# The 96-column matmuls of the 96 + 32 expert units issued as three of 32 columns

## The chip, the cores and the metric

The kernel runs on one core of a Trainium2 chip. The metric is the device time of one execution in microseconds, as the median of several runs.

## The reference, cut to what matters

One layer of a diffusion backbone: 512 latent tokens and 256 context tokens of width 1024 go through a modulated norm, an input projection, two scans (SSD and mLSTM) in both directions and an output projection; then the latent tokens alone go through a mixture of 32 experts, of which each token uses two. The change touches the experts only:

```
g_sel = jnp.argmax(g_logits, axis=-1)                      # one group of 8 experts per token
top_logit, top_idx = lax.top_k(e_logits, MOE_TOP_K)        # two experts inside it
...
hidden = silu(einsum("td,edf->tef", t, w_gate[lo:hi])) * einsum("td,edf->tef", t, w_up[lo:hi])
hidden = hidden * combine[:, grp, :, None]
y = y + einsum("tef,efd->td", hidden, w_down[lo:hi])
```

An expert is a gate and an up matrix of 1024 x 256 each and a down matrix of 256 x 1024, all in float32.

## The kernel before

After the scans and the router, the kernel knows how many tokens each expert has. It ranks the experts by that, and gives them places in 14 units of 128 rows (`plan`, line 40, `SEQ_U`, line 59): a P or M unit holds two experts with 64 rows each, a B unit one with 128, a C unit two with 96 and 32, a Q unit four with 32 each. The order is P P P M C B M C Q B M C Q Q, units 0 to 13; a table says which token stands in which row, and rows that stay empty give nothing. Tokens that find no place go through a loop of extra tiles (line 1331), which runs as often as it is needed.

The loop over the units (line 1410) does the following for each. POOL gathers the 128 token rows into `xg` (line 1413). The unit's experts' weights are tiles `we` of 128 x 2048 float32, 1 MB, three to an expert: two hold gate and up for half of the depth each, the third the down matrix. `load_unit` (line 931) issues them on SP's queue, through `piece` (line 908), in the order first tiles, second tiles, third tiles of all the unit's experts. There are 20 slots for such tiles; a load waits until the slot's last reader is done, and until the load two before it has landed. So SP runs ahead of PE by up to 20 tiles. The last unit's down matrices come in narrower pieces (`piece_cols`, line 922).

Line 1416 makes `halves`: for each expert of the unit a triple of its weight tiles, the first of its rows and their number. `moe_tile` (line 1263) then computes the unit. PE transposes `xg` (tile `xt`, line 1269); DVE and ACT scale it into `xT` (tokens along the columns). For each of the eight blocks k of the depth, and for each entry of `halves`, one matmul (line 1279) takes the entry's columns of `xT` as the stationary operand and 512 columns of its weight tile as the moving one, and adds into the entry's rows of `gu`: gate on the left, up on the right. ACT and DVE make `hid` of it, PE transposes that, and the down matmuls (line 1313, tile `yy`) go in the same way over two halves of the output and two blocks q of the hidden width, again one for each entry of `halves`. Every float32 matmul shows in the trace as two instructions with two weight loads. DVE scales the result (`yf`), ACT and DVE split it into `yH` and `yL`, and the scatter matmuls (lines 1299 and 1300, tile `pa`) with a one-hot matrix bring the rows back to token order, where DVE adds them to `x1t`. PE does the scatter of one unit between the matmuls of the next.

Of the kernel before, what the change touches and what calls it, by code (L numbers as in the profile page):

```python
# [82 lines left out]
def body(tc, a, out, dbg=None):  # L83
# [28 lines left out]
    def mps(name):  # L112
        return pmix.tile([128, 512], F32, name=name, tag="mx", bufs=3)
# [526 lines left out]
    for c in (5, 4, 3, 2, 1, 0):  # L640
        o = (c % 4) * 128
# [289 lines left out]
    def load_unit(es, last):  # L931
        ws = [[None] * 3 for _ in es]
        for t in range(3):
            for w, e in zip(ws, es):
                w[t] = piece(e, t, LASTC if last and t == 2 else None)
        if last:
            for c0, cn in LASTC:
                for w, e in zip(ws, es):
                    piece_cols(w[2], e, c0, cn)
        return ws  # L940
# [238 lines left out]
    def gather(xg, idx):  # L1179
        G.indirect_dma_start(out=xg, out_offset=None, in_=xnd, in_offset=bass.IndirectOffsetOnAxis(ap=idx, axis=0), bounds_check=SEQ - 1, oob_is_err=False)  # L1180
# [78 lines left out]
    def onehot(n, tokf):  # L1259
        oh_ = mw.tile([128, SEQ], F32R, name=f"oh{n}", tag="oh", bufs=1)  # L1260
        return oh_, ts(oh_, iota, tokf, None, ALU.is_equal)
# [65 lines left out]
    def rank_exp(r):  # L1327
        return SY.value_load(ordi[0:1, r:r + 1], min_val=0, max_val=NE - 1)
# [81 lines left out]
    for i, unit in enumerate(UNITS):  # L1410
        oh_ = None
        if i:
            gather(xgs[0], tabi[:, i:i + 1])
            oh_ = onehot(i, tabf[:, i, 0:1])[0]
        ws = [pre[r] for r, _, _ in unit] if unit[0][0] < NP else load_unit([rank_exp(r) for r, _, _ in unit], i == NU - 1)
        halves = [(w.__getitem__, p0, m) for w, (_, p0, m) in zip(ws, unit)]
        if i == NU - 1:
            fw = slots[npc[0] % NSLOT][0].tile([128, 2048], F32, name="fw", tag="we", bufs=1)
            fwr = fw[0:1, D:2 * D]
            S.dma_start(fwr, a["fw"])  # L1420
            for nb in range(2):
                pf_ = mps(f"pfw{nb}")
                T.matmul(pf_, ones[0:1], fwr[:, nb * 512:nb * 512 + 512], start=True, stop=True)
                S.copy(fw[:, nb * 512:nb * 512 + 512], pf_)
        moe_tile(i, xgs[0], oh_, tabf[:, i, 1:2], halves, last=i == NU - 1)
# [85 lines left out]
```

## Time and profile before

| | us |
|---|---|
| median of 3 runs | 796.37 |
| lowest, highest | 796.34, 801.81 |
| span of the profiled execution | 795.4 |
| of it PE busy with matmuls | 729.2 |
| DVE busy | 411.7 |
| ACT busy | 267.2 |
| POOL busy | 139.5 |
| mean granted clock of PE | 0.970 of full speed |

The profiled span goes from the first to the last instruction of one execution; it lies 1.0 us below the median of the timed runs. The expert stage fills the time from about 455 us to the end. "PE" is the matmuls, "PEld" their weight loads, which can run beside them; "SPq" is what SP's DMA queue issues. In a shape such as `128*96 128x512`, 128 is the depth of the matmul, 96 the number of stationary columns (rows of the result), and 512 the moving columns.

### The profile page before, as it was taken

The numbers are of one execution on the slowest core, as the hardware profiler recorded it, in microseconds if no ns is written. First come the engines' busy times: TensorE is split into PE (matmuls) and PEld (weight loads), VectorE is DVE, ScalarE is ACT, GpSimd is POOL, SyncE is SP. The second block draws the span as 40 slices with busy tenths as digits, with TensorE's granted clock in tenths as the row PEclk, the third lists the DMA queues.
The fourth block names the chain that finished last, engine by engine and source line by source line (L and its number), as shares of the span: only waits on it lengthen the run. The fifth ranks groups of instructions, "written<-read, shape, count | busy, mean of one in ns | idle before, by whom it ended". The sixth has DMA issues, their size and how long they took to land.

```text
span 795.4 us, 10678 instructions
## 1 busy us (share of the span) xinstructions
PE 729.2 (92%) x3941; PEld 427.2 (54%) x3941; DVE 411.7 (52%) x872; ACT 267.2 (34%) x576; POOL 139.5 (18%) x142
## 2 busy tenths in 40 slices
PE   5998999999989999999989578999999999999883
PEld 3554544446768888999978433333343234323321
DVE  3557594124565757349886834444353245434415
ACT  6235215212644684642444411221122112202224
POOL 3110000201386420136560100000000000000002
PEclk9999999999999999999999779999999999999997
DMA  8765367210514831152485579988668579893722
GB/s 354 251 240 226 131 214 267 70 36 31 183 52 165 306 139 54 54 207 87 162 314 246 214 298 399 362 320 316 241 220 333 216 268 340 318 386 131 270 101 105
DMA packets 36648, 171.59 MB, mean 216 GB/s; under 512 B 4643, under 2 KB 7283, under 8 KB 23796
## 3 DMA queue, kind: packets, MB, share of 16 engines
q1 hardware_dynamic: 32912, 162.68, 55.0%
q0 software_dynamic: 2592, 6.30, 2.2%
q10 hardware_dynamic: 1092, 1.93, 0.8%
q8 instruction: 31, 0.51, 0.2%
q14 instruction: 21, 0.17, 0.1%
HBM read 169.74 MB, written 4.30 MB: 219 GB/s over the span
## 4 chain that ended last, share of the span: by engine, by line
PE 82%; DVE 7%; ACT 5%; issue 2%; POOL 2%; DMA 1%; another core or an unknown queue 0%; SPq 0%; DVEq 0%; ACTq 0%; POOLq 0%
PE gu L1279 17%; PE sx L256 10%; PE yy L1313 10%; PE z L256 5%; PE pa L1299 4%; PE pa L1300 3%; PE o L256 3%; PE op L256 3%; PE oq L256 3%; PE xm L256 2%; PE v L256 2%; PE py L704 2%; PE modl L578 2%; PE xm_c L256 1%; PE mod L277 1%
## 5 line engine op out<-in xcount | busy, mean ns | idle before, releaser
L1279 PE MATMUL gu<-we,xT 128*32 128x512 f32 (+3 forms) x512 | 140.9, 620 | 1.0 <-DVE xT L121 1.0
L116 DVE TENSOR_TENSOR x1t<-x1t,pa 128x512 f32<-128x512 f32 (+1 forms) x116 | 72.0, 665 | 44.4 <-PE pa L1300 44.4
L1313 PE MATMUL yy<-we,hTm 128*32 128x512 f32 (+4 forms) x272 | 80.2, 592 | 1.9 <-ACT hTm L1291 1.0
L1279 PEld LDWEIGHTS gu<-we,xT 128*32 128x32 f32 (+3 forms) x512 | 35.5, 132 | 82.7 <-issue 79.8
L1180 POOL DMA_INDIRECT xg<-xnd,tabi x14 | 14.2, 1013 | 266.3 <-PE xt L1269 243.6
L1299 PE MATMUL pa<-yH,oh 128*128 128x512 f32 (+1 forms) x116 | 47.7, 468 | 3.3 <-ACT yH L1318 2.6
L1284 ACT ACTIVATE hid<-gu 128x256 f32<-128x256 f32 x14 | 5.4, 384 | 124.7 <-PE gu L1279 124.7
L1318 ACT CAST yH<-yf 128x512 fp32r<-128x512 f32 (+1 forms) x29 | 17.5, 603 | 86.0 <-DVE yf L116 86.0
L1313 PEld LDWEIGHTS yy<-we,hTm 128*32 128x32 f32 (+3 forms) x272 | 20.6, 130 | 46.0 <-issue 39.3
L124 DVE SCALAR_TENSOR_TENSOR hid<-hid,tabf,gu 128x256 f32<-128x256 f32 x14 | 6.7, 480 | 72.6 <-ACT hid L1284 72.6
L124 DVE SCALAR_TENSOR_TENSOR cv<-sx,pc,cv 128x510 f32<-128x510 f32 (+1 forms) x32 | 23.8, 744 | 30.3 <-ACT cv L454 29.8
L1300 PE MATMUL pa<-yL,oh 128*128 128x512 f32 (+1 forms) x116 | 39.4, 397 | 0.0
L1275 ACT ACTIVATE xT<-xt,mv,mv 128x128 f32<-128x128 f32 x84 | 32.1, 455 | 20.0 <-DVE xT L121 20.0
L1299 PEld LDWEIGHTS pa<-yH,oh 128*128 128x128 f32 x116 | 20.4, 188 | 33.0 <-ACT yH L1318 12.4
L116 DVE TENSOR_TENSOR yf<-yy,g2b 128x512 f32<-128x512 f32 (+1 forms) x29 | 19.4, 670 | 35.8 <-PE yy L1313 35.5
L226 POOL TENSOR_TENSOR w_1L<-w,w_1H 128x1024 fp32r<-128x1024 f32 x5 | 12.1, 2424 | 131.7 <-ACT w_1H L222 131.7
L1319 DVE TENSOR_TENSOR yL<-yf,yH 128x512 fp32r<-128x512 f32 (+1 forms) x29 | 19.5, 672 | 13.0 <-ACT yH L1318 12.9
L1300 PEld LDWEIGHTS pa<-yL,oh 128*128 128x128 f32 x116 | 20.5, 188 | 9.0 <-DVE yL L1319 3.1
L1269 PE MATMUL xt<-ident,xg 128*128 128x128 f32 x112 | 19.6, 289 | 4.4 <-issue 4.4
L692 ACT ACTIVATE sg<-sg,cu 128x128 f32<-128x128 f32 x64 | 19.6, 389 | 9.1 <-POOL sg L629 9.1
L226 POOL TENSOR_TENSOR w_0L<-w,w_0H 128x1024 fp32r<-128x1024 f32 x3 | 7.2, 2412 | 86.4 <-ACT w_0H L222 86.4
L256 PE MATMUL sx<-hH,w_0H 128*128 128x512 f32 x32 | 19.5, 620 | 3.1 <-DVE cv L124 2.0
(515 smaller groups left out, 1701.6 us busy)
## 6 DMA issues: line engine op xcount, KB each, us to landing
we<-in_wex_dram SPq DMA_DIRECT2D x92, 1024.0 KB, 6.0
wl<-in_w_mod_dram SPq DMA_DIRECT2D x16, 1024.0 KB, 5.2
w<-in_win_dram SPq DMA_DIRECT2D x24, 512.0 KB, 6.5
wm<-in_wm_dram SPq DMA_DIRECT2D x8, 1024.0 KB, 10.1
sg<-rowS SPq DMA_DIRECT2D x8, 512.0 KB
sw<-rowS SPq DMA_DIRECT2D x8, 512.0 KB, 7.8
xin<-in_x_dram SPq DMA_DIRECT2D x4, 512.0 KB
mg<-rowM SPq DMA_DIRECT2D x4, 512.0 KB
```

Of the source, the lines that this page charges most:

```text
L116: return (eng or V).tensor_tensor(o, x, y, op)
L124: return V.scalar_tensor_tensor(o, x, s, y, o1, o2)
L226: wsub[0] = G.tensor_tensor(wL, raw, wH, ALU.subtract)
L256: T.matmul(ps, l, r, start=(start and i == 0), stop=(stop and i == n - 1))
L692: S.activation(gb[:, h], gb[:, h], AF.Exp, bias=cu[:, c, 12 * d + h:12 * d + h + 1])
L1269: T.transpose(pt[:, q * 128:(q + 1) * 128], xg[:, k * 128:(k + 1) * 128], ident)
L1275: S.activation(xT[:, k], pt[:, q * 128:(q + 1) * 128], AF.Identity, bias=B2[:, k:k + 1], scale=A2[:, k:k + 1])
L1279: T.matmul(gu[p0:p0 + m], xT[:, k, p0:p0 + m], w(k // 4)[:, (k % 4) * 512:(k % 4) * 512 + 512], start=(k == 0), stop=(k == KB - 1))
L1299: T.matmul(pa, osl, yH, start=True, stop=False)
L1300: T.matmul(pa, osl, yL, start=False, stop=True)
L1313: T.matmul(py[p0:p0 + m], hT[:, q, p0:p0 + m], w(2)[:, q * D + c0:q * D + c0 + cn], start=(q == 0), stop=(q == 1))
L1319: V.tensor_sub(yL, yf, yH)
```

## The change

Line 1416 makes more entries for `halves`. An expert with 96 rows in its unit (only the first of a C unit has that) gives three entries of 32 rows, at its first row and at 32 and 64 rows behind it, all with the same weight tiles. Experts with 128, 64 or 32 rows give one entry as before. `moe_tile` is not changed: it issues one matmul for each entry, at lines 1279 and 1313.

```
-        halves = [(w.__getitem__, p0, m) for w, (_, p0, m) in zip(ws, unit)]
+        halves = [(w.__getitem__, p0 + o, min(m, q_)) for w, (_, p0, m) in zip(ws, unit) for q_ in ((32 if m == 96 else 128),) for o in range(0, m, q_)]
```

## Rows read from the trace of the kernel before

**Rows 1.** The page, part 1: engine, busy us (share of the span), instructions.

```profile
PE 729.2 (92%) x3941; PEld 427.2 (54%) x3941; DVE 411.7 (52%) x872; ACT 267.2 (34%) x576; POOL 139.5 (18%) x142
```

**Rows 2.** Chain of waits from 455 us on, shares by line.

```profile
by line: PE gu L1279 40.0%; PE yy L1313 22.7%; PE pa L1299 9.0%; PE pa L1300 7.9%; PE xt L1269 2.6%; DVE hid L124 2.0%; PE ph L1288 1.9%; issue 1.7%; ACT hTm L1291 1.6%; ACT hid L1284 1.5%; DVE yf L116 1.1%; another core or an unknown queue
```

**Rows 3.** Timeline, PE: first `gu` rows of units; start, us, line, tiles, shape, count.

```profile
544.09 5.03 PE L1279 MATMUL gu<-we,xT 128*96 128x512 f32 x10
...
574.28 2.74 PE L1279 MATMUL gu<-we,xT 128*128 128x512 f32 x6
...
611.24 5.03 PE L1279 MATMUL gu<-we,xT 128*96 128x512 f32 x10
...
641.52 2.76 PE L1279 MATMUL gu<-we,xT 128*32 128x512 f32 x18
...
661.18 2.74 PE L1279 MATMUL gu<-we,xT 128*128 128x512 f32 x6
...
698.16 5.03 PE L1279 MATMUL gu<-we,xT 128*96 128x512 f32 x10
...
728.44 1.06 PE L1279 MATMUL gu<-we,xT 128*32 128x512 f32 x6
...
751.17 1.04 PE L1279 MATMUL gu<-we,xT 128*32 128x512 f32 x2
```

**Rows 4.** Timeline, PE's weight loads inside unit 4, a C unit.

```profile
557.89 0.24 PEld L1279 LDWEIGHTS gu<-we,xT 128*96 128x96 f32 x2 [0.84 <-issue]
558.92 0.14 PEld L1279 LDWEIGHTS gu<-we,xT 128*32 128x32 f32 x2 [0.78 <-issue]
559.89 0.24 PEld L1279 LDWEIGHTS gu<-we,xT 128*96 128x96 f32 x2 [0.84 <-issue]
```

**Rows 5.** Timeline, PE's weight loads inside unit 8, a Q unit.

```profile
648.37 0.13 PEld L1279 LDWEIGHTS gu<-we,xT 128*32 128x32 f32 x4 [0.30 <-issue]
...
648.79 0.13 PEld L1279 LDWEIGHTS gu<-we,xT 128*32 128x32 f32 x4 [0.30 <-issue]
```

**Rows 6.** Chain of waits in order of time: start, us, what; units 4, 8.

```profile
544.25 4.87 PE gu L1279 x10
...
550.51 2.00 PE gu L1279 x4
552.98 9.01 PE gu L1279 x18
...
563.91 7.11 PE yy L1313 x14
...
641.60 2.69 PE gu L1279 x18
...
645.89 0.99 PE gu L1279 x8
...
647.55 4.51 PE gu L1279 x38
...
653.99 3.62 PE yy L1313 x26
```

**Rows 7.** Line 1279, its weight loads: min/median/max in ns, starts, shapes.

```profile
L1279 PEld LDWEIGHTS gu<-we,xT x512: 106/136/230, 462.6 to 765.1; 128*32 128x32 f32 x80, 128*64 128x64 f32 x65, 128*96 128x96 f32 x16, 128*128 128x128 f32 x10
```

**Rows 8.** Line 915, the weight tiles' loads from issue to landing.

```profile
DMA to landing us min/median/max: 4.8/6.0/9.0
```

**Rows 9.** Timeline: SP's queue over two stretches, and `yy` of unit 12.

```profile
704.00 42.09 SPq L915 DMA_DIRECT2D we<-in_wex_dram  x9
...
704.00 11.64 SPq L915 DMA_DIRECT2D we<-in_wex_dram  x5
...
741.75 1.91 PE L1313 MATMUL yy<-we,hTm 128*32 128x512 f32 x8
```

**Rows 10.** Waits of SP's queue: us in total, times, longest.

```profile
SPq L915 <- DMA fw<-in_fw_dram: 22.2, 1, 22.2
```

**Rows 11.** Window table: stretch, its us, each engine's busy us, clock, DMA, GB/s.

```profile
757.00:762.00 5.00, 5.00 (x29) 1.27 (x32) 0.00 (x0) 0.77 (x2) 0.00 (x0) 0.66 0.89 300
```

## The prediction

> **What bounds the kernel now.** The page's busy times come first: PE is busy for 729.2 of the 795.4 us, and nothing else comes near it [rows 1]. A busy share alone proves little, so the chain of waits is read next, for the expert stage alone (455 us to the end): PE's gate/up matmuls (`gu`, line 1279) are 40.0% of it, the down matmuls (`yy`, line 1313) 22.7%, the scatter matmuls 16.9%; DVE and ACT appear with one or two per cent each, a DMA of weights not at all [rows 2]. So in this stage a microsecond of PE is a microsecond of the kernel, as long as the weights are there.
>
> Third comes the timeline, cut at the first `gu` matmul of each unit [rows 3]. The 14 units run in the order P P P M C B M C Q B M C Q Q. The three C units (96 + 32 columns) are units 4, 7 and 11. Their spans, first `gu` to the next unit's first `gu`: 574.28 - 544.09 = 30.19, 641.52 - 611.24 = 30.28, 728.44 - 698.16 = 30.28 us. Unit 8 is a Q unit: four experts of 32 columns, the same 128 tokens, the same depth, twice the weight bytes. It takes 661.18 - 641.52 = 19.66 us. C does the same arithmetic on fewer weights and takes 10.6 us longer.
>
> Fourth, the weight loads of PE inside the units say why. In C, the load for a 96-column matmul, the load for the 32-column one and the next 96 start at 557.89, 558.92 and 559.89 [rows 4]: 1.03 us for the 96, then 0.97 us for the 32, one after the other, 2.00 us for one step (one k of `gu`). Every fp32 matmul here is two instructions, so this step is four. In Q, four loads start at 648.37 and the next four at 648.79 [rows 5]: four matmul instructions of 32 columns pass side by side in 0.43 us (0.42 by these two rows, rounded up), 0.86 us for a step of two passes. The 96 and the 32 do not overlap; four 32s do.
>
> **The change, part by part.** *Removed:* in each C unit 16 `gu` and 8 `yy` instructions of 96 columns. *Added:* three times as many of 32 columns, with the same tokens' columns cut in three and the same weight tile for all three. The fourth 32 is as before. Per C unit that makes 64 `gu` and 32 `yy` instructions in place of 32 and 16: exactly the count, the shapes and the weight loads of a Q unit. For the kernel it is 3 x 48 = 144 more matmuls and as many more loads: 4085 of each in place of 3941 [rows 1].
>
> *The price by step.* A C unit has 8 `gu` steps and 4 `yy` steps (two halves of the output, two q each), 36 in three units. From 2.00 to 0.86 us each that would be 36 x 1.14 = 41.0 us, an upper bound: matmuls that are cut off from their group by a scatter matmul pay for a whole pass, and Q pays that too. *By the chain's pieces:* `gu` took 4.87 + 2.00 + 9.01 = 15.88 us in unit 4 and 2.69 + 0.99 + 4.51 = 8.19 in unit 8, the long `yy` piece 7.11 against 3.62 [rows 6]; 7.69 + 3.49 = 11.2 us for a unit, 33.5 for three. *By spans,* which leave nothing out: 30.19 - 19.66 = 10.53 and twice 30.28 - 19.66 = 10.62, in sum 31.8 us. I take the spans: they hold every gap, and everything that DVE, ACT and POOL do in a unit (the scaling, the splitting of the result, the scatter adds) is the same in C and Q, so what of it isn't hidden under a shorter `gu` already stands in Q's 19.66.
>
> *What the trace doesn't show.* Nowhere before do three matmuls in different column groups read one and the same weight tile at once; in Q and in the 64 + 64 units each has its own tile. The bounds: nothing, that is Q's 0.86 us a step; or the three take turns and only the fourth goes beside them, 3 x 0.86 = 2.58 us a step, 0.58 more than now. I take Q's value, because a C step then differs from a Q step only in three start addresses, and in Q the four streams are already read apart from each other.
>
> *The cover: weights in time.* A shorter unit asks for its weights sooner. A load takes 6.0 us to land, by its median [rows 8]. The last nine full loads issue from 704.00 to 745.76 (704.00 + 42.09 less the last one's own 0.33); unit 13 has eight of them, so unit 12's last is the one at 704.00 [rows 9] and lands at about 710.0. Its first use is `yy` of unit 12, at 741.75 [rows 9]: 31.7 us to spare. By then PE will be 31.8 us ahead. Even if no load came earlier, unit 12 would wait 0.1 us; unit 13's fourth (the last of the five that start with 704.00, so issued at 715.3, landed at 721.3, wanted at 751.17 [rows 3, 9]) has 29.9 to spare, and waits 1.9 us at worst. Loads do come earlier, since each waits for a slot that a unit gives back. So: nothing, at most 1.9 us. Unit 13's last three full loads are held up for 22.2 us by the load of the final norm's weights [rows 10], which waits for a slot of unit 12; that chain follows unit 12 and moves with it.
>
> *A rule against the change.* By rows 5, the weight loads of a Q step lie under the matmuls: a load starts with every pass, yet the passes stay 0.43 apart. The Trainium skill, "TensorE: Matmul & The Clock Gate", section "Part 3: Packing small matmuls — row/col tiling", says that a weight load overlaps with running matmuls only where their row groups differ; here all four use all 128 rows, so by that rule the added loads would stand in the open. The trace speaks against it; what it would cost is the second rival.
>
> *Sum.* 795.4 - 31.8 = 763.6 us of span. The profiled span lies 1.0 below the median of the runs (796.37), so 796.4 - 31.8 = 764.6 us.
>
> **The rivals.**
> (1) *The gain is partly given back to a stall between units.* Unit 12, a Q unit too, takes 751.17 - 728.44 = 22.73 us [rows 3], 3.1 more than unit 8: there PE takes the scatter of the unit before sooner and waits for ACT and DVE to split the result. If all three C units fall into that order, 9.3 us go: 773.9. For it: unit 12 shows it. Against: units 7 and 8 do not, and C's count of steps is unit 8's.
> (2) *Half the overlap.* If weight loads are not hidden, a step pays 8 x 0.106 us, the shortest load [rows 7], 0.85 + 0.86 = 1.71 us; if the matmuls on one tile pass two at a time, 1.72. Either saves 0.29 x 36 = 10.4 us: 786. Q's rows speak against the first, nothing but Q's likeness against the second.
> (3) *Slower: matmuls on one weight tile take turns.* 2.58 us a step, 0.58 x 36 = 20.9 us more: 817. It decides from a step of 2.00 us on, 2.3 times Q's; at about 2.00 the change does nothing and the time stays at 796.
> (4) *More than forecast.* Fewer steps cut in two by scatter matmuls, and unit 12's 3.1 us or a clock dip gone: between 757 and 762 us the granted clock was 0.66 [rows 11], part of the time at 1.2 in place of 2.4 GHz, after a stretch in which PE waited; that is worth 5 x 0.34 = 1.7 us. 31.8 + 3.1 + 1.7 = 36.6: 759.8; the step bound gives 755.4.
>
> **How the numbers follow.** Forecast 0.75 (its own range 761 to 770: the chain's sum 33.5 and the clock dip on one side, 1.9 us of weights and one stall of 3.1 on the other); (1) 0.10; (2) 0.05; (3) 0.05 slower and 0.02 at no change; (4) 0.03. The range leaves out (2) and (3): 757 to 775. About 1% is what a measurement can tell here, some 8 us: faster takes the forecast, (1), (2) and (4), 0.93; same 0.02; slower 0.05.
>
> **What the profile after would show.** Right: 4085 PE instructions, no form of 96 columns left, C spans of 19 to 21 us, four weight loads in every 0.43 us in a C unit, P, M, B and Q units as long as before, SP without a new wait that PE feels. Wrong: steps of C above 0.9 us (rivals 2, 3), waits of PE on `yH` after a C unit (rival 1), PE waiting for a `we` load in units 12 or 13 (the weights' cover gone).

## The result, and the profile after

The changed kernel takes 764.38 us (median of 4 runs, 764.18 to 766.52) against 796.36 (the median with a fourth run of the kernel before); the ratio is 0.956, with a 95% interval of 0.951 to 0.961. The forecast was 764.6.

The page of the changed kernel, part 1, in the columns of [rows 1]: 144 matmuls and weight loads more, 33.4 us less of PE, the other engines as before.

```profile
PE 695.8 (91%) x4085; PEld 420.5 (55%) x4085; DVE 411.5 (54%) x872; ACT 266.9 (35%) x576; POOL 139.7 (18%) x142
```

PE's timeline after, the first `gu` row of units 4, 5, 7, 8, 11, 12 and 13, as in [rows 3]:

```profile
544.94 2.76 PE L1279 MATMUL gu<-we,xT 128*32 128x512 f32 x18
...
564.54 2.74 PE L1279 MATMUL gu<-we,xT 128*128 128x512 f32 x6
...
601.63 2.76 PE L1279 MATMUL gu<-we,xT 128*32 128x512 f32 x18
...
621.33 2.76 PE L1279 MATMUL gu<-we,xT 128*32 128x512 f32 x18
...
678.11 2.76 PE L1279 MATMUL gu<-we,xT 128*32 128x512 f32 x18
...
697.80 1.91 PE L1279 MATMUL gu<-we,xT 128*32 128x512 f32 x10
...
719.92 1.04 PE L1279 MATMUL gu<-we,xT 128*32 128x512 f32 x2
```

The C units now take 564.54 - 544.94 = 19.60, 621.33 - 601.63 = 19.70 and 697.80 - 678.11 = 19.69 us, where they took 30.19, 30.28 and 30.28: 31.8 us less. Unit 8, the Q unit that served as the model, takes 19.7 as before.

Inside unit 4, PE's weight loads after (compare [rows 4] and [rows 5]):

```profile
551.76 0.13 PEld L1279 LDWEIGHTS gu<-we,xT 128*32 128x32 f32 x4 [0.30 <-issue]
552.19 0.13 PEld L1279 LDWEIGHTS gu<-we,xT 128*32 128x32 f32 x4 [0.30 <-issue]
```

Four loads in every 0.43 us, three of the four matmuls on one weight tile: one pass for all four, to the same hundredth as in the Q unit. The chain of waits after, in order of time, has for unit 4 the pieces that [rows 6] has for unit 8:

```profile
545.01 2.69 PE gu L1279 x18
...
549.29 0.99 PE gu L1279 x8
...
550.95 4.48 PE gu L1279 x38
...
557.36 3.62 PE yy L1313 x26
```

8.16 us of `gu` in place of 15.88, and 3.62 in place of 7.11 for the long `yy` piece.

The weights' cover: SP's queue from the load that is unit 12's last, `yy` of unit 12 that first wants it, and the loads' time to land.

```profile
680.81 34.10 SPq L915 DMA_DIRECT2D we<-in_wex_dram  x9
...
710.50 1.91 PE L1313 MATMUL yy<-we,hTm 128*32 128x512 f32 x8
...
DMA to landing us min/median/max: 4.9/5.7/8.8
```

Issued at 680.81, landed by about 686.5 (the median), wanted at 710.50: 24 us to spare, against 31.7 before [rows 8, 9]. PE is 31 us earlier at that place, the load 23 us. PE's matmuls show no wait for a weight tile; on the side of the weight loads the waits view has a little, 0.8 us in three places:

```profile
PEld gu L1279 <- DMA we<-in_wex_dram: 0.8, 3, 0.4
```

**The whole difference of the two spans**, 795.4 - 762.5 = 32.9 us, by the rows of both: the first C unit starts 0.85 us later (544.94 against 544.09); the three C units give 31.76; units 5 and 6 (from 564.54 to 601.63) and 8 to 10 (from 621.33 to 678.11) take 0.13 and 0.14 us more; unit 12 takes 719.92 - 697.80 = 22.12, 0.61 less; from the start of unit 13 to the end it is 42.6 instead of 44.2, 1.6 less. In sum -32.9. The last term is the clock. The timeline has the same 60 `gu` instructions of unit 13 in 8.76 us before and in 7.06 after; the window table, in the columns of [rows 11], has for that part now:

```profile
757.35 8.76 PE L1279 MATMUL gu<-we,xT 128*32 128x512 f32 x60
...
726.10 7.06 PE L1279 MATMUL gu<-we,xT 128*32 128x512 f32 x60
...
725.00:730.00 5.00, 5.00 (x42) 1.40 (x43) 0.38 (x1) 1.17 (x2) 0.00 (x0) 1.00 1.03 354
```

A granted clock of 1.00 (2.4 GHz throughout) where it was 0.66 (part of the time 1.2 GHz). This is no effect of the change: unit 13 takes 42.5 to 42.6 us in all the profiles that follow but the last experiment's, with 96 + 32 columns too; only the profiled execution of the kernel before had 44.2. PE had waited just ahead of it in both executions (0.56 and 0.43 us before, 0.56 and 0.42 after), so what made the clock fall in one of them is not shown.

### The profile page after: what moved, and what is told of

It reads as the page before. It is cut to its first block, busy times and chain, and to the rows that moved or that the text cites. A ratio compares the mean times of both kernels' runs of the same rounds, so it can differ in the third digit from the quotient of the medians.

```text
span 762.5 us, 10966 instructions
## 1 busy us (share of the span) xinstructions
PE 695.8 (91%) x4085; PEld 420.5 (55%) x4085; DVE 411.5 (54%) x872; ACT 266.9 (35%) x576; POOL 139.7 (18%) x142
## 4 chain that ended last, share of the span: by engine, by line
PE 79%; DVE 8%; ACT 5%; issue 2%; DMA 2%; POOL 2%; another core or an unknown queue 0%; DVEq 0%; SPq 0%; ACTq 0%; POOLq 0%
PE gu L1279 15%; PE sx L256 11%; PE yy L1313 9%; PE z L256 6%; PE pa L1299 4%; PE pa L1300 4%; PE o L256 3%; PE oq L256 3%; PE xm L256 3%; PE op L256 2%; PE modl L578 2%; PE xm_c L256 2%; PE v L256 1%; PE py L704 1%; PE mod L277 1%
## 5 line engine op out<-in xcount | busy, mean ns | idle before, releaser
L1279 PE MATMUL gu<-we,xT 128*32 128x512 f32 (+2 forms) x608 | 116.0, 602 | 1.0 <-DVE xT L121 1.0
L1313 PE MATMUL yy<-we,hTm 128*32 128x512 f32 (+3 forms) x320 | 69.8, 590 | 1.9 <-ACT hTm L1291 1.0
L1279 PEld LDWEIGHTS gu<-we,xT 128*32 128x32 f32 (+2 forms) x608 | 31.9, 123 | 61.3 <-issue 57.3
L1299 PE MATMUL pa<-yH,oh 128*128 128x512 f32 (+1 forms) x116 | 45.4, 445 | 2.5 <-ACT yH L1318 1.8
L1313 PEld LDWEIGHTS yy<-we,hTm 128*32 128x32 f32 (+2 forms) x320 | 19.1, 123 | 36.9 <-issue 30.2
L1269 PEld LDWEIGHTS xt<-ident,xg 128*128 128x128 f32 x112 | 13.9, 147 | 15.3 <-issue 13.7
## 6 DMA issues: line engine op xcount, KB each, us to landing
wm<-in_wm_dram SPq DMA_DIRECT2D x8, 1024.0 KB, 10.2
```

What stands on the lines that cost most here:

```text
L1269: T.transpose(pt[:, q * 128:(q + 1) * 128], xg[:, k * 128:(k + 1) * 128], ident)
L1279: T.matmul(gu[p0:p0 + m], xT[:, k, p0:p0 + m], w(k // 4)[:, (k % 4) * 512:(k % 4) * 512 + 512], start=(k == 0), stop=(k == KB - 1))
L1299: T.matmul(pa, osl, yH, start=True, stop=False)
L1313: T.matmul(py[p0:p0 + m], hT[:, q, p0:p0 + m], w(2)[:, q * D + c0:q * D + c0 + cn], start=(q == 0), stop=(q == 1))
```

## The experiments

All are edits of the changed kernel, except `e2_no_alternation`. They ran in two groups, each on one chip: beside the first four the kernel before took 798.33 us, beside the last four 801.22. So their times are read as ratios, and their causes as spans of units, from the first `gu` of one to that of the next.

The question is why C is fast now. My theory: matmuls pass side by side only where they are of one width and in different columns of the array; each change of width waits for what runs. The rivals: it was only that 96 is no good width; it was the alternation of widths that cost the time; or the added instructions have a price of their own that C's gain hides.

### 64 + 32 beside 32

```
- ... for q_ in ((32 if m == 96 else 128),) for o in range(0, m, q_)]
+ ... for o, n in (((0, 64), (64, 32)) if m == 96 else ((0, m),))]
```

> The changed kernel, but the 96 rows are cut in 64 + 32 beside the 32 of the other expert: three entries of unlike width in three places that do not touch. Theory (only matmuls of one width pass side by side; a change of width waits for the matmuls before): a step is one pass pair for the 64 (0.86 us) and one for the two 32s (0.86) with two changes of width (0.28 together, 2.00 - 2 x 0.86): about 2.0 us, no better than 96 + 32, so C units near 30 us and 796 us. Rival (any column groups that do not touch pass side by side, and 96 is merely no width of the array): 0.86 us a step, C units near 19.7 us and 764 us.

Measured: 799.08 us, ratio to before 1.001 (0.998 to 1.004). The timeline of this run gives a C unit as 575.40 - 544.72 = 30.68 us, and its weight loads show the step:

```profile
544.72 5.04 PE L1279 MATMUL gu<-we,xT 128*64 128x512 f32 x14
...
575.40 2.74 PE L1279 MATMUL gu<-we,xT 128*128 128x512 f32 x6
```

```profile
556.89 0.19 PEld L1279 LDWEIGHTS gu<-we,xT 128*64 128x64 f32 x2 [0.84 <-issue]
557.89 0.14 PEld L1279 LDWEIGHTS gu<-we,xT 128*32 128x32 f32 x4 [0.81 <-issue]
558.88 0.19 PEld L1279 LDWEIGHTS gu<-we,xT 128*64 128x64 f32 x2 [0.84 <-issue]
```

The 64 runs for itself, 1.00 us; then the two 32s together, 0.99 us. 64 and 32 are widths that pass side by side with their own kind elsewhere in this kernel (a unit of 64 + 64 takes 19.7 us, as one of four 32s does, see the run with P and M units in 32s), their columns do not touch, and still they take turns. The rival that only 96 is at fault falls: the whole gain needs equal widths.

### All of the 96 first, then all of the 32

The kernel before, with the loops turned round in C units:

```
-        for k in range(KB):
-            for w, p0, m in halves:
+        ap = [m for _, _, m in halves] == [96, 32]
+        for k, (w, p0, m) in [(k, h) for h in halves for k in range(KB)] if ap else [(k, h) for k in range(KB) for h in halves]:
...
-            qw = ... if last else ...
+            qw = ... if last or ap else ...
```

> The kernel before, 96 + 32 as it was, but in the C units all 96-column matmuls of a group come first and all 32-column ones after them (in gu over all eight k, in yy over both q): the change of width falls once to a group, not twice to a step. Theory (a step of 2.00 us is 0.86 for the 96, 0.86 for the 32 and 0.28 for two changes of width, and the larger part of the gain comes from passing side by side): 36 steps save about 0.28 each, 10 us less than before, some 786 us. Rival (the cost is nearly all in the change of width): near the changed kernel, 764 us. Rival (no cost in the change of width): 796 us.

Measured: 788.15 us, ratio 0.987 (0.981 to 0.992). Timeline: a C unit takes 571.93 - 544.26 = 27.67 us, 2.5 less than before. Weight loads of the 32s, two of the run:

```profile
544.26 2.74 PE L1280 MATMUL gu<-we,xT 128*96 128x512 f32 x6
...
571.93 2.74 PE L1280 MATMUL gu<-we,xT 128*128 128x512 f32 x6
```

```profile
553.51 0.11 PEld L1280 LDWEIGHTS gu<-we,xT 128*32 128x32 f32 x1 [0.32 <-issue]
553.94 0.11 PEld L1280 LDWEIGHTS gu<-we,xT 128*32 128x32 f32 x1 [0.32 <-issue]
```

One 32 now goes in every 0.43 us, alone; without the alternation it no longer pays the change of width, but it has the whole pass to itself. So of the 10.6 us of a C unit about 2.5 are the changes of width that this run takes away, and the other 8, by subtraction, are mostly matmuls side by side. I had put 3.4 us (12 x 0.28) on the changes; one to a group is left, and those around the scatter matmuls. That the total still came near the 786 us expected is in part luck: the three C units give 7.6 of the 10 us, and 1.7 of the 9.1 us between the profiled spans (795.4 and 786.3) are unit 13 without the fall of the clock.

### `gu` alone

```
+        wide = [(w.__getitem__, p0, m) for w, (_, p0, m) in zip(ws, unit)]
...
- ... else [(q, h) for q in range(2) for h in halves]
+ ... else [(q, h) for q in range(2) for h in wide or halves]
```

> The changed kernel, but the yy matmuls of the C units are 96 + 32 as before; only gu is cut in 32s. Theory (each group gains by its own steps): of 10.6 us for a C unit, gu gives 7.4 (its span falls from 17.88 to 10.43 us) and yy with what follows 3.2, so three units give back 9.5 us: about 774 us. Rival (the two do not add, because the scatter work after yy needs its time anyway): nearer 764 us.

Measured: 778.83 us (774.11 to 779.9), ratio 0.972 (0.966 to 0.979). Timeline, unit 4 and the start of unit 5:

```profile
550.25 2.76 PE L1279 MATMUL gu<-we,xT 128*32 128x512 f32 x18
...
562.67 7.11 PE L1313 MATMUL yy<-we,hTm 128*96 128x512 f32 x14
...
573.05 2.74 PE L1279 MATMUL gu<-we,xT 128*128 128x512 f32 x6
```

573.05 - 550.25 = 22.80 us: 7.4 less than before, 3.2 more than with both, as the theory's sum has it. `yy` takes its old 7.11 us. The two parts add. The median is 5 us above the 774 expected; in the profiled execution (779.08) that lies ahead of the stage, whose first `gu` starts at 468.82 us, 5.7 later than in the changed kernel's; from there to the end it takes 308.6 us, 9.2 more than the changed kernel's 299.4, where 9.5 was expected.

### B units cut in 32s too

```
- ... for q_ in ((32 if m == 96 else 128),) ...
+ ... for q_ in ((32 if m in (96, 128) else 128),) ...
```

> The changed kernel, and in the two B units the 128-column matmuls are four of 32 columns with one weight tile too: the same steps of 0.86 us, four times the instructions. Theory (cutting costs nothing by itself, but scatter matmuls of another width that fall into a group cost whole passes and changes of width, as in the units of 32 and 64): a B unit goes from 16.5 us to a Q unit's 19.7, so about 6 us slower than the changed kernel, 771 us. Rival (a matmul of 32 costs no more than a quarter of one of 128 in every place): 764 us. Rival (four on one weight tile pass more slowly than three and another): beyond 775 us.

Measured: 774.88 us, ratio 0.970 (0.964 to 0.976). A B unit takes 590.86 - 571.16 = 19.70 us here, 16.54 (581.08 - 564.54, its neighbour's first `gu` row) in the changed kernel; the M unit behind it takes 19.74, not 20.55. Twice 3.16 - 0.81 = 2.35 makes 4.7 us, not the 6 I expected: I had left out the unit behind. The first `gu` row is that of a Q unit to the hundredth (18 instructions in 2.76 us), so four 32s on one weight tile pass no more slowly than three and another: that rival falls.

```profile
571.16 2.76 PE L1279 MATMUL gu<-we,xT 128*32 128x512 f32 x18
...
590.86 2.79 PE L1279 MATMUL gu<-we,xT 128*64 128x512 f32 x10
```

```profile
581.08 1.07 PE L1279 MATMUL gu<-we,xT 128*64 128x512 f32 x2
```

(The second fence is the changed kernel's timeline.) The rest of the 774.88 does not come from the experts. The first `gu` starts at 469.89 us in this run and at 463.21 in the repeat of the changed kernel (`c1_changed_again` below), though the work ahead of it is the same. The chain of waits splits these 6.7 us at the start of `oq`, matmuls of the output projection ahead of the router; the repeat, this run, and the last run of this document (`e6_whole_steps`):

```profile
410.89 8.66 PE oq L256 x36
...
414.55 8.64 PE oq L256 x36
...
414.15 8.66 PE oq L256 x36
```

From there to the first `gu` it is 52.3 us in the repeat and 55.3 in this run: 3.0 us, in a stretch in which the window tables show that the clock fell, this run first, then the repeat:

```profile
435.00:445.00 10.00, 10.00 (x60) 8.78 (x60) 6.00 (x27) 4.41 (x9) 0.55 (x1) 0.81 0.18 73
...
435.00:445.00 10.00, 10.00 (x64) 8.37 (x63) 7.38 (x37) 3.89 (x9) 1.50 (x2) 1.00 0.44 154
```

The other 3.7 us are there when `oq` starts. The clock alone does not explain them: `e6_whole_steps` comes to the same place 3.3 us late, 2.2 of them later than 334 us, with a granted clock of 1.00 from 340 to 414 us. There the chain runs over two loads of weights `wp` (3.65 and 4.00 us) and DVE's work on them, in the repeat over one such load (3.74 us) and PE; why the order differs is open. So the stage alone is read from here on: 773.5 - 469.9 = 303.6 us in this run.

### The changed kernel again

> The changed kernel once more, beside the next three on one chip. Every theory: about 764 us, C units 19.6 to 19.7 us; what differs from that lies ahead of the expert stage or in the clock.

Measured: 765.76 us (764.23 to 771.01), ratio 0.959 (0.952 to 0.965); the expert stage is 762.5 - 463.2 = 299.3 us, as in the result's profile (762.5 - 463.1 = 299.4).

### P and M units in 32s

```
- ... for q_ in ((32 if m == 96 else 128),) ...
+ ... for q_ in ((32 if m in (96, 64) else 128),) ...
```

> The changed kernel, and the 64-column matmuls of the P and M units are two of 32 columns each: 6 units with twice the matmul instructions and weight loads, 288 matmuls more. Theory (a step costs 0.86 us whether two of 64 or four of 32 fill it, and the added loads lie under the matmuls): no change, 764 us, P and M units 19.5 to 19.7. Rival (added instructions and loads cost something each, and the B units of e4_b_in_32s grew for that reason): by that run's 3.1 us for a unit, some 15 us more, near 780 us.

Measured: 767.43 us (763.83 to 768.98), ratio 0.959 (0.953 to 0.965), the same as the repeat beside it. The stage takes 762.1 - 463.3 = 298.8 us. The page has 288 matmuls and loads more, and PE is no busier; units 2 and 3 (timeline) take 525.15 - 505.43 = 19.72 and 544.88 - 525.15 = 19.73 us, in the changed kernel 19.71 and 19.72:

```profile
PE 694.9 (91%) x4373; PEld 417.7 (55%) x4373; DVE 411.9 (54%) x872; ACT 266.9 (35%) x576; POOL 140.2 (18%) x142
```

```profile
505.43 2.76 PE L1279 MATMUL gu<-we,xT 128*32 128x512 f32 x18
...
525.15 2.76 PE L1279 MATMUL gu<-we,xT 128*32 128x512 f32 x18
...
544.88 2.76 PE L1279 MATMUL gu<-we,xT 128*32 128x512 f32 x18
```

So the added matmuls and their loads have no price where they fill the same passes, and the B units of the run before did not grow for their number. What they did pay is the next question: a unit of matmuls 128 wide is 3 us shorter than one of the same number of steps in narrow ones. The supposition is that the scatter matmuls, 128 wide too, cut into it without a change of width and without leaving part of a step behind; in narrow groups they can be made to cut less. The next two runs test that.

### `yy` not cut by the scatter

```
-            if last and nb == 0:
+            if nb == 0:
                 continue
             scatter(*todo.pop(0))
```

> The changed kernel, but the scatter of the first output half comes after all yy matmuls of the unit, not before the last of them. Theory (a group that scatter matmuls cut inside a step pays a whole pass pair and a change of width for what is left over: the last yy pair took 1.0 us by itself): about 1.0 us less for each of the 10 units whose yy is cut now (three P, three M, three C, unit 8), 754 us; C units 18.7. Rival (PE's time is only moved, since the scatter then waits for DVE and ACT): 764 us.

Measured: 754.25 us, ratio 0.944 (0.937 to 0.950). Timeline, unit 4 and the start of unit 5:

```profile
539.92 1.04 PE L1279 MATMUL gu<-we,xT 128*32 128x512 f32 x2
...
552.34 3.64 PE L1313 MATMUL yy<-we,hTm 128*32 128x512 f32 x32
...
558.41 1.02 PE L1279 MATMUL gu<-we,xT 128*128 128x512 f32 x2
```

All 32 `yy` instructions take 3.64 us, where 26 of them took 3.62 and the other six another 0.99 behind the scatter. The C unit is 558.41 - 539.92 = 18.49 us, 1.1 less; the stage, 751.9 - 462.7 = 289.2 us, is 10.2 shorter. The work was not only moved. The 754 expected was met, but not unit by unit: unit 8 takes 19.68 us and gained nothing. In this order its `gu` is cut three times, into 2, 6, 2 and 54 instructions, where that of a C unit is cut into 2, 8 and 54:

```profile
612.59 1.04 PE L1279 MATMUL gu<-we,xT 128*32 128x512 f32 x2
...
614.23 1.06 PE L1279 MATMUL gu<-we,xT 128*32 128x512 f32 x6
...
615.88 1.04 PE L1279 MATMUL gu<-we,xT 128*32 128x512 f32 x2
```

Two left-over instructions cost as much as six: that is the price of a cut inside a step. The B units, as wide as the scatter matmuls, take 16.54 us as before.

### `gu` cut between whole steps only

In addition, the scatter of a unit's second half is written into the next unit's `gu`, three pairs behind the third k and the fourth behind the fifth, in fixed order on PE (and a unit's one-hot matrix is made after its `gu`, not before it, since the scatter still uses the one before):

```
+    pend, CUT = [], {2: (0, 3), 4: (3, 4)}
...
+            if pend and k in CUT:
+                tail = pend[0](*pend[1], rng=CUT[k], after=gm_)
...
+        if not last and n < 100:
+            pend.extend((scatter, todo.pop(0)))
```

> As e5_yy_whole, and the scatter of the second output half stands in the next unit's gu between whole steps: three scatter pairs after the third k, the fourth after the fifth. Theory (gu cut inside steps pays one more pass pair, 0.86 us, and it needs its changes of width either way): another 0.9 us or so for each unit whose gu is cut inside a step (P, M, C and Q units but the first, some ten), near 745 us; C units under 18 us. Rival (PE then waits where the scatter is not ready, because its order is fixed): no gain over e5_yy_whole, or a loss.

Measured: 749.29 us (745.37 to 755.28), ratio 0.936 (0.928 to 0.944), the best of all kernels here. Timeline, unit 4 and the start of unit 5:

```profile
542.58 2.78 PE L1284 MATMUL gu<-we,xT 128*32 128x512 f32 x24
...
546.88 1.92 PE L1284 MATMUL gu<-we,xT 128*32 128x512 f32 x16
...
549.39 2.78 PE L1284 MATMUL gu<-we,xT 128*32 128x512 f32 x24
...
560.25 2.74 PE L1284 MATMUL gu<-we,xT 128*128 128x512 f32 x6
```

The pieces are whole steps now (24, 16 and 24 instructions, eight to a step). The unit takes 560.25 - 542.58 = 17.67 us, 0.8 less than in the run before, and the stage 748.5 - 466.5 = 282.0, 7.2 less. The B units stay at 16.5 us. Its time of 749.29 is above the 745 I expected mostly because the first `gu` starts at 466.48, some 3 to 4 us later than in most runs; the stage alone is 17.4 us shorter than the changed kernel's 299.4, where I expected about 19.

## Why the prediction was right

**The bound.** PE's matmuls set the expert stage, and a microsecond taken from them came off the end: 31.8 us in the C units, 32.0 between the medians.

**The price by spans.** The term that carried the sum, a C unit becomes a Q unit of 19.66 us, was right to 0.06 us in each of the three. The bound by steps, 41.0 us, was not reached, and the last two runs show where most of the rest lies (5.8 of 9.2 us): in steps that scatter matmuls cut, and in changes of width around them. With whole steps the same unit takes 17.67 us, 12.5 less than the 30.19 at the start; the three together 37.6 us.

**The unknown.** Three streams from one weight tile pass with the fourth in 0.42 to 0.43 us: the free end of the bounds. Rival 3 (taking turns) and both halves of rival 2 (loads in the open, two at a time) are refuted by that spacing. In 64 + 32 + 32, two 32s on two tiles share a slot of 0.99 us as well.

**Why 96 + 32 took turns** was only read off before; the run with 64 + 32 + 32 shows it as a matter of unlike widths (1.99 us a step, 2.00 with 96 + 32), the run without alternation prices the changes of width apart (2.5 us of 10.6 a unit). The Trainium skill, "TensorEngine Tiling (Array Packing)", section "Key Properties", says that changing the tiling mode drains the engine; the trace fits that, with 0.11 to 0.17 us a change (0.97 and 1.03 in place of 0.86, [rows 4]). That matmuls of two widths don't run at one time, even in columns that don't touch, is what the 1.99 us add to it.

**The rule against the change.** The added loads stay under the matmuls: four in each 0.43 us, and 288 more of them in the P and M units left the stage at 298.8 us against 299.3. Nor does the length of a load show: in the run without alternation one matmul goes in every 0.43 us with a load of 0.11 us (32 columns) and with one of 0.16 us (96), in the B units with one of 0.19 us (128). So the rule of "TensorE: Matmul & The Clock Gate", section "Part 3: Packing small matmuls — row/col tiling", in the Trainium skill, that loads overlap with running matmuls only across row groups, does not hold in this kernel, where all use all 128 rows; the measurement decides.

**The weights' cover.** No unit lost time to weights that a span shows: 24 us to spare for unit 12's last load, where the least possible was 0.1 us short. The loads did come earlier, as slots came back earlier.

**What was off, and cancelled.** The profiled span shrank by 32.9 us, 1.1 more than the sum: 1.6 from the clock in unit 13, which the change did not cause, and 0.6 from unit 12, where PE no longer waits for `yH` at its start, both of rival 4, less 0.85 ahead of the first C unit and 0.3 between. On the other side, I put 1.0 us around the span, by the median; the execution profiled after took 764.18 for a span of 762.5, 1.7 us. The forecast is within 0.2 us partly by that luck; its own range of 761 to 770 is the better measure of what was known. Rival 1 (a stall between units) did not come. The waits view of the changed kernel has three waits of PE for `yH`; the timeline puts them at 717, 739 and 748 us, in units 12 and 13, none behind a C unit:

```profile
PE pa L1299 <- ACT yH L1318: 1.8, 3, 0.7
```

## What to carry to other kernels

In a kernel whose time PE's matmuls set: those of 32 columns shared a pass with others of 32, those of 64 with 64, and neither 96 with 32 nor 64 with 32 did (float32, 512 moving columns). So cut a group so that its pieces are all as wide as the narrowest, even if several then read one and the same moving tile, and count passes, not instructions. Then keep such a group whole: a 128-wide matmul that slips in between the matmuls of a step leaves a part that costs as much as a whole step (1.04 us for two instructions), and moving the scatter out of the steps was worth another 17 us of the stage here. Before a stretch is forecast by a step's price, look for a stretch in the same trace that already has the shapes it will have; its span holds what a sum of steps leaves out.

## What the runs showed of the hardware that was not expected

The granted clock differed between executions on the same instructions: 0.81 against 1.00 from 435 to 445 us in one run, 0.66 against 1.00 in unit 13 of the kernel before, with 3.0 us lost around the first stretch and 1.7 in the second. The start of the stage moved between 462.6 and 469.9 us, and in part without the clock, as the work on the `wp` weights came in another order. A comparison of less than 1% in this kernel has to be read from spans inside the trace.
